# Softmax shift by a scaled minimum, and four order edges between attention and gMLP, in a one-core encoder block

## Chip, core and metric

The kernel runs on one core of one Trainium2 chip. The metric is the device time of one execution in microseconds (us), lower is better. PE is TensorE (matrix products; PEld its weight loads), DVE is VectorE, ACT is ScalarE, POOL is GpSimd; SP is SyncE, which here only issues transfers.

## What is computed

One layer of an encoder on a sequence of 512 positions and 1024 features, in float32. The change touches the attention branch and the gMLP branch. The reference, cut to these:

```python
n = rms_norm(h, norm_mix_pre)
z_gmlp, q, k, v, gates = jnp.split(n @ w_in, split_points, axis=-1)
# gMLP: z -> gelu(z) = [u | v]; LN(v); mixing of positions in chunks of 128
y_a = gmlp_spatial_gating(jax.nn.gelu(z_gmlp), ...)          # u * (W_s LN(v) + b_s)
# attention: 3 groups (dilation 1, 4, 16) of 4 heads, windows of radius 64
s = jnp.einsum('bdnqhe,bdnkhe->bdnhqk', qb, kw) * scale
s = jnp.where(valid, s, MASK_VALUE)
m = jnp.max(s, axis=-1, keepdims=True)
p = jnp.exp(s - m)
denom = jnp.sum(p, axis=-1, keepdims=True)
o = jnp.einsum('bdnhqk,bdnkhe->bdnqhe', p, vw) / denom
lse = (m + jnp.log(denom))[..., 0]
w_mix = jax.nn.softmax(jnp.stack(lses, axis=0), axis=0)      # mixes the 3 groups
y_b = jnp.sum(w_mix[..., None] * o_all, axis=0)
...                                                          # gates, W_out, then the feed-forward part
```

## The kernel before

Every float32 operand of a large product is split in two fp32r halves, `hi` (a copy by ACT) and `lo = x - hi` (a subtraction by DVE), and a product is three matmuls (`mm3`, L94 to L98): hi x hi, hi x lo, lo x hi. `wsplit` (L72 to L79) splits a block of weights; its ACT line is L77 and its DVE line L78. `split_into` (L90 to L92) does the same for activations; `dma_split` (L81 to L88) forms `lo` with two ACT copies and an accumulating transfer issued by POOL.

The stages, in the order of the program:

- Norm of the input, then the attention values of three groups (`token_major`, L267; the tiles `pv` are its four accumulators, 128 positions each).
- Four heads (L671 to L673): `project_qk(h)` and then `mix(h)`. `project_qk` projects q and k for the three groups. `seven_qk` (L424) does it by a seven-product scheme: products 6, 1, 5, 2, 7, 3, 4 of 12 matmuls each into three half banks X, Y, Z, with copies between them: `p1` (ACT, L439) reads X after product 1, `u2` (DVE, L445) adds Y and p1, `z5` (ACT, L447) reads Z, `u3` (DVE, L451) reads Y. Product 2 adds into X, 7 into Y, 3 into Z, so they come after these reads. Then rotary positions (`rotate`), scores (`scores_a` for group 0, `scores_b` for groups 1 and 2 together) and softmax.
- `softmax_tile` (L526 to L533) treats one tile of 128 rows and 256 keys: one DVE operation adds the mask and takes the row maximum `mx` (L529), a second, of one column, forms `nm = -SCALE * mx` (L531), and ACT computes `exp(SCALE * s + nm)` with its row sum (L532). A head has 4 tiles "a" and 4 tiles "b".
- `mix(h)` (L562 to L606) combines the groups: with the row maxima and sums of both kinds it computes factors on a few columns. Two small matmuls with a constant matrix (`pp`, L569, and `pc`, L592) carry numbers between row orders. ACT then scales the four "b" tiles (L598) and, with `ca` (L596), the four "a" tiles (`scale_a`, L602). For heads 0 to 2 `scale_a` is traced during the next head's first `seven_qk` (list `pending`), for the last head at once.
- `attend(h)` transposes the scaled probabilities (L625, L638) and multiplies them with the values into `py` (L655 to L657, L662). It is traced in the middle of the next head. The result of heads 0 to 2 goes to memory (`ybd`, L669) and is loaded back after the heads (`ybh`, `ybl`, L681).
- gMLP: `token_major(COL_V, ...)` (L726) projects the gMLP's values into four accumulators `pv` (8 k x 4 r x 3 = 96 matmuls of 512 columns); their evacuation `evac_v` (L716 to L724) is `gelu2` (ACT square L692, DVE L693, ACT tanh L694, DVE L695), statistics, a power on POOL (`rs_out`, L108) and the normalisation `vln` (L724). Then u (tiles `pf`, L737) is projected group by group, with the steps of the last head's `attend` in between (L728 to L741), and gated with the mixed values (`pg`, L749).
- Gates, branches and W_out, and then the feed-forward part, which is some two thirds of the time.

The order of the instructions on each engine is not that of the program. A scheduler orders them ahead of time with its own estimate of durations, each engine's queue is then fixed, and on the chip each engine works through its queue in that order, waiting for what an instruction needs. `tc.issue_after(x)` adds edges to that: instructions traced inside the block that run on x's engine are put behind x in that engine's queue. It adds no wait on the chip. Transfers issued by POOL or SP stand in those queues as well.

Two buffers matter. The half banks X, Y, Z and the accumulators `pv` come from the same four banks ("acc"), so that the first `pv` matmuls share PE with the last head's projections. And the weight blocks `slab` (the value weights, two of 1 MB), `uw` (u) and `gw` (gates) share three buffers ("raw"), so that a load waits until an earlier block has been split.

Of the kernel before, what the change touches and what calls it, by code (L numbers as in the profile page):

```python
# [10 lines left out]
F32 = mybir.dt.float32  # L11
F32R = mybir.dt.float32r
AF = mybir.ActivationFunctionType
ALU = mybir.AluOpType
PSUM = bass.MemoryType.PSUM

P = 128
S = 512
D = 1024
KD = D // P  # L20
# [4 lines left out]
NH = 4  # L25
SCALE = 1.0 / math.sqrt(HD)
NEG = -1e30
GW = 512
COL_U, COL_V = 0, GW
COL_Q, COL_K, COL_VV, COL_G = 1024, 2560, 4096, 5632  # L30
ROT = 64
# [6 lines left out]
def block_kernel(ctx: ExitStack, tc: tile.TileContext, x, norm_mix_pre, w_in, b_gate, ln_v_gain, ln_v_bias,  # L38
                 w_spatial, b_spatial, w_branch_a, w_branch_b, w_out, norm_mix_post, norm_mlp_pre, w_up,
                 w_down, norm_mlp_post, rope_c, mask_c, perm_c, out):  # L40
    nc = tc.nc
# [30 lines left out]
    def wsplit(raw, pl=None, bufs=None, tag="w", sub=None):  # L72
        pl = pl or wpool
        shape = list(raw.shape)
        hi = pl.tile(shape, F32R, name="hi", tag=tag + "hi", bufs=bufs)
        lo = pl.tile(shape, F32R, name="lo", tag=tag + "lo", bufs=bufs)
        nc.scalar.activation(hi, raw, AF.Copy)  # L77
        (sub or nc.vector).tensor_tensor(lo, raw, hi.bitcast(F32), op=ALU.subtract)  # L78
        return hi, lo  # L79
# [14 lines left out]
    def mm3(ps, a, b, start, stop):  # L94
        (ah, al), (bh, bl) = a, b
        nc.tensor.matmul(ps, ah, bh, start=start, stop=False)  # L96
        nc.tensor.matmul(ps, ah, bl, start=False, stop=False)  # L97
        return nc.tensor.matmul(ps, al, bh, start=False, stop=stop)  # L98
# [38 lines left out]
    start = ExitStack()  # L137
# [126 lines left out]
        for k0 in range(0, nk, kper):  # L264
            yield k0, wload([kper, ncol], lambda r: [(r, wap[k0 * P:(k0 + kper) * P, c0:c0 + ncol].rearrange("(k p) c -> p k c", p=P))], "slab")

    def token_major(c0, stationary, evac, half_way=None):  # L267
        accs = [psA.tile([P, 512], F32, name="pv", tag="acc", bufs=4) for _ in range(4)]
        for k0, raw in slabs(w_in, c0, KD, 512, 4):
            if k0 and half_way:  # L270
                half_way()
            for j in range(0, 4, 2):
                wh, wl = wsplit(raw[:, j:j + 2])
                for jj in range(2):
                    k = k0 + j + jj
                    for r in range(4):
                        mm3(accs[r], (stationary(nh, k, r), stationary(nl, k, r)), (wh[:, jj], wl[:, jj]), k == 0, k == KD - 1)
        for r in range(4):
            evac(r, accs[r])

# [245 lines left out]
    def softmax_tile(h, ab, i, ps, mask):  # L526
        mx = stat[h, "m", ab]
        p = ppool.tile([P, 2, P], F32, name="p")
        nc.vector.tensor_tensor_reduce(p, ps, mask, 1.0, -3.0e38, ALU.add, ALU.max, mx[:, i:i + 1])  # L529
        nm = small.tile([P, 1], F32, name="nm", bufs=8)  # L530
        nc.vector.tensor_scalar(nm, mx[:, i:i + 1], -SCALE, None, op0=ALU.mult)  # L531
        nc.scalar.activation(p, p, AF.Exp, bias=nm, scale=SCALE, accum_out=stat[h, "d", ab][:, i:i + 1])  # L532
        probs[h, ab, i] = p  # L533

    def scores_b(h, got):
# [26 lines left out]
    def mix(h):  # L562
        mda, mdb = stat[h, "md", "a"], stat[h, "md", "b"]
        shape = [P, 2, 4, 4]
        xa = small.tile(shape, F32, name="xa", bufs=2)
        nc.vector.tensor_tensor(xa, mda.unsqueeze(3).to_broadcast(shape), by_r.to_broadcast(shape), op=ALU.mult)
        bank = {"tag": "S", "bufs": 2} if h == NH - 1 else {"tag": "T"}
        pp = psA.tile(shape, F32, name="pp", **bank)
        nc.tensor.matmul(pp, perm[:, 0:P], xa, start=True, stop=True)  # L569
        xb = small.tile(shape, F32, name="xb", bufs=2)  # L570
        nc.vector.tensor_tensor(xb, pp, by_c.to_broadcast(shape), op=ALU.mult)
        mab = small.tile([P, 2, 4], F32, name="mab", bufs=2)
        nc.vector.tensor_reduce(mab, xb.rearrange("p m c r -> p m r c"), axis=mybir.AxisListType.X, op=ALU.add)
        big = small.tile([P, 4], F32, name="big", bufs=2)
        nc.vector.tensor_tensor(big, mab[:, 0], mdb[:, 0], op=ALU.max)
        e = small.tile([P, 2, 4], F32, name="e", bufs=2)
        nc.vector.tensor_tensor(e[:, 0], mab[:, 0], big, op=ALU.subtract)
        nc.vector.tensor_tensor(e[:, 1], mdb[:, 0], big, op=ALU.subtract)
        nc.scalar.activation(e, e, AF.Exp, scale=SCALE)
        z = small.tile([P, 2, 4], F32, name="z", bufs=2)  # L580
        nc.vector.tensor_tensor(z[:, 0], e[:, 0], mab[:, 1], op=ALU.mult)
        nc.vector.tensor_tensor(z[:, 1], e[:, 1], mdb[:, 1], op=ALU.mult)
        nc.vector.tensor_tensor(z[:, 0], z[:, 0], z[:, 1], op=ALU.add)
        nc.vector.reciprocal(z[:, 0], z[:, 0])
        cf = small.tile([P, 2, 4], F32, name="cf", bufs=2)
        nc.vector.tensor_tensor(cf[:, 0], e[:, 0], z[:, 0], op=ALU.mult)
        nc.vector.tensor_tensor(cf[:, 1], e[:, 1], z[:, 0], op=ALU.mult)
        sq = [P, 1, 4, 4]
        xc = small.tile(sq, F32, name="xc", bufs=2)
        nc.vector.tensor_tensor(xc, cf[:, 0:1].unsqueeze(2).to_broadcast(sq), by_c.to_broadcast(sq), op=ALU.mult)  # L590
        pc = psA.tile(sq, F32, name="pc", **bank)
        nc.tensor.matmul(pc, perm[:, P:2 * P], xc, start=True, stop=True)  # L592
        xd = small.tile(sq, F32, name="xd", bufs=2)
        nc.vector.tensor_tensor(xd, pc, by_r.to_broadcast(sq), op=ALU.mult)
        ca = small.tile([P, 4], F32, name="ca", bufs=2)
        nc.vector.tensor_reduce(ca, xd[:, 0], axis=mybir.AxisListType.X, op=ALU.add)  # L596
        for i in range(4):
            nc.scalar.activation(probs[h, "b", i], probs[h, "b", i], AF.Copy, scale=cf[:, 1, i:i + 1])  # L598

        def scale_a():  # L600
            for i in range(4):
                nc.scalar.activation(probs[h, "a", i], probs[h, "a", i], AF.Copy, scale=ca[:, i:i + 1])  # L602
        if h == NH - 1:
            scale_a()
        else:
            pending.append(scale_a)  # L606

    def attend(h):
        for _ in attend_steps(h):
# [80 lines left out]
    def gelu2(ps, dst):  # L690
        t = gpool.tile([P, S], F32, name="gt", bufs=2)
        nc.scalar.activation(t, ps, AF.Square)  # L692
        nc.vector.scalar_tensor_tensor(t, t, 1.0 / GELU_A, ps, op0=ALU.add, op1=ALU.mult)  # L693
        nc.scalar.activation(t, t, AF.Tanh, scale=GELU_C * GELU_A)  # L694
        nc.vector.scalar_tensor_tensor(dst, t, 1.0, ps, op0=ALU.add, op1=ALU.mult)  # L695
# [19 lines left out]

    def evac_v(c, ps):  # L716
        v = vln[:, c]
        gelu2(ps, v)
        st6 = small.tile([P, 6], F32, name="st6")
        nc.vector.bn_stats(st6, v)  # L720
        mv = small.tile([P, 2], F32, name="mv")
        nc.vector.bn_aggr(mv, st6)
        r = rstd_of(mv[:, 1:2], 1.0, 4.0 * EPS)
        normed.append(nc.vector.tensor_scalar(v, v, mv[:, 0:1], r, op0=ALU.subtract, op1=ALU.mult))  # L724

    token_major(COL_V, lambda n, k, c: n[:, k, ROT + c * P:ROT + (c + 1) * P], evac_v)  # L726

    steps = attend_steps(NH - 1, "S", 2)  # L728
    next(steps)
    for g2 in range(2):  # L730
        raw = wload([KD, 2 * P], lambda r: [(r, fcols(w_in, COL_U + g2 * 2 * P, KD, 2 * P))], "uw")
        for j in range(2):
            g = 2 * g2 + j
            wh, wl = dma_split(raw[:, :, j * P:(j + 1) * P], fcols(w_in, COL_U + g * P, KD, P))
            ps = psA.tile([P, S], F32, name="pf", tag="acc" if g else "T", bufs=4 if g else 1)
            for k in range(KD):
                ins = mm3(ps, (wh[:, k], wl[:, k]), (nhn[:, k], nln[:, k]), k == 0, k == KD - 1)  # L737
                if k % 4 == 3 and steps:
                    with tc.issue_after(ins.ins):
                        if next(steps, 0) == 0:  # L740
                            steps = None  # L741
            u = gpool.tile([P, S], F32, name="u", bufs=2)
            gelu2(ps, u)
            if g == 0:
                with tc.issue_after(ins.ins):
                    spatial_weights()
            pg = psA.tile([P, 4, P], F32, name="pg", tag="acc", bufs=4)
            for c in range(4):
                nc.tensor.matmul(pg[:, c], vln[:, c, g * P:(g + 1) * P], wst[:, g], start=True, stop=True)  # L749
            t = gpool.tile([P, 4, P], F32, name="sv")  # L750
            nc.vector.scalar_tensor_tensor(t, pg, cols[:, 16 + g:17 + g], sbias[:, g:g + 1].to_broadcast([P, 4, P]), op0=ALU.mult, op1=ALU.add)
            tf = t.rearrange("p c t -> p (c t)")
            nc.vector.scalar_tensor_tensor(tf, tf, 0.5, u, op0=ALU.mult, op1=ALU.mult)
            split_into(yah[:, g], yal[:, g], tf)
# [585 lines left out]
```

## Time and profile before

| | us |
|---|---|
| median of 3 runs | 775.78 (775.67 to 775.94) |
| profiled execution | 775.82 |
| its span, first to last instruction | 774.0 |
| PE busy | 765.8 (99%) |
| PEld busy | 693.1 (90%) |
| DVE busy | 606.7 (78%) |
| ACT busy | 470.2 (61%) |
| POOL busy | 106.3 (14%) |

The span is shorter than the execution's time by what lies around it (1.8 us). A PE that is busy is not one at its peak: matmuls are pipelined, and how far apart they start depends on their shape and on what stands before them. In rows of the order of time each line gives start, duration, engine, source line, operation, output <- input and, in brackets, the idle time before it and what ended it. In rows of waits: who waited <- for whom: total us, times, longest. In rows of the chain: start, us, what. Starts of PE rows differ by 0.15 us between the order of time and the chain, since the chain counts a matmul from where it takes over the array.

### The profile page before, as it was taken

The numbers are of one execution on the slowest core, as the hardware profiler recorded it, in microseconds if no ns is written. First come the engines' busy times: TensorE is split into PE (matmuls) and PEld (weight loads), VectorE is DVE, ScalarE is ACT, GpSimd is POOL, SyncE is SP. The second block draws the span as 40 slices with busy tenths as digits, with TensorE's granted clock in tenths as the row PEclk, the third lists the DMA queues.
The fourth block names the chain that finished last, engine by engine and source line by source line (L and its number), as shares of the span: only waits on it lengthen the run. The fifth ranks groups of instructions, "written<-read, shape, count | busy, mean of one in ns | idle before, by whom it ended". The sixth has DMA issues, their size and how long they took to land.

```text
span 774.0 us, 12492 instructions
## 1 busy us (share of the span) xinstructions
PE 765.8 (99%) x4903; PEld 693.1 (90%) x4903; DVE 606.7 (78%) x976; ACT 470.2 (61%) x766; POOL 106.3 (14%) x148
## 2 busy tenths in 40 slices
PE   9999999999999999999999999999999999999996
PEld 6888999999998889999998899999999988888885
DVE  7784689888883888778766459998888699978785
ACT  6352468978778674545453557566666766655671
POOL 3300200010103440001000210011211100203010
PEclk9999999999999999999999999999999999999999
DMA  9743744262557993224446323469999988979702
GB/s 311 247 123 113 200 109 110 58 167 77 134 167 138 248 185 83 82 83 135 146 146 209 128 94 124 163 198 290 197 275 223 239 308 308 197 248 213 217 1 108
DMA packets 104348, 131.63 MB, mean 170 GB/s; under 512 B 3393, under 2 KB 73825, under 8 KB 103394
## 3 DMA queue, kind: packets, MB, share of 16 engines
q1 hardware_dynamic: 75472, 79.31, 32.0%
q0 software_dynamic: 28528, 51.15, 28.7%
q8 instruction: 38, 0.62, 0.3%
q10 hardware_dynamic: 290, 0.40, 0.1%
q14 instruction: 20, 0.16, 0.1%
HBM read 120.87 MB, written 26.74 MB: 191 GB/s over the span
## 4 chain that ended last, share of the span: by engine, by line
PE 96%; DMA 2%; DVE 1%; issue 0%; POOL 0%; ACT 0%; POOLq 0%; DVEq 0%; ACTq 0%
PE pacc L1063 13%; PE pg L378 12%; PE pgacc L378 7%; PE pd L1156 6%; PE pd L1154 6%; PE pd L1155 6%; PE ptp L1063 5%; PE pf L96 4%; PE pf L97 4%; PE pf L98 4%; PE pv L97 4%; PE pv L98 4%; PE pv L96 4%; PE pgS L378 3%; PE pd L97 2%; PE pd L96 2%
## 5 line engine op out<-in xcount | busy, mean ns | idle before, releaser
L1155 PE MATMUL pd<-hl,hhl 128*128 128x512 f32 x224 | 87.2, 389 | 0.0
L1156 PE MATMUL pd<-hl,hhl 128*128 128x512 f32 x224 | 87.0, 389 | 0.0
L1154 PE MATMUL pd<-hl,hhl 128*128 128x512 f32 x224 | 84.7, 389 | 0.0
L1063 PE MATMUL pacc<-nt,hl 128*128 128x256 f32 x504 | 66.1, 279 | 0.0
L1063 PEld LDWEIGHTS pacc<-nt,hl 128*128 128x128 f32 x504 | 62.0, 188 | 0.1
L77 ACT ACTIVATE hi<-s 128x1024 fp32r<-128x1024 f32 x34 | 35.9, 1059 | 36.7 <-DVE s L362 11.7
L1156 PEld LDWEIGHTS pd<-hl,hhl 128*128 128x128 f32 x224 | 42.0, 188 | 8.8
L1155 PEld LDWEIGHTS pd<-hl,hhl 128*128 128x128 f32 x224 | 42.0, 188 | 8.8
L78 DVE TENSOR_TENSOR lo<-s,hi 128x1024 fp32r<-128x1024 f32 x34 | 41.5, 1224 | 10.6 <-ACT hi L77 10.3
L1154 PEld LDWEIGHTS pd<-hl,hhl 128*128 128x128 f32 x224 | 42.0, 188 | 8.6
L91 ACT ACTIVATE hl<-s 128x1024 fp32r<-128x1024 f32 x28 | 29.4, 1057 | 26.0 <-DVE s L1046 18.7
L92 DVE TENSOR_TENSOR hl<-dnw,hl 128x1024 fp32r<-128x1024 f32 x32 | 38.5, 1223 | 7.5 <-ACT hl L91 7.5
L1063 PE MATMUL pacc<-n,hl 128*128 128x256 f32 x336 | 44.1, 279 | 0.0
L91 ACT ACTIVATE hl<-dnw 128x1024 fp32r<-128x1024 f32 x32 | 33.0, 1054 | 18.0 <-DMA dnw<-in_w_down_dram 5.6
L1063 PEld LDWEIGHTS pacc<-n,hl 128*128 128x128 f32 x336 | 41.3, 188 | 0.0
L378 PE MATMUL pg<-nt,hi 128*128 128x256 f32 x216 | 39.8, 281 | 0.0
L92 DVE TENSOR_TENSOR hl<-s,hl 128x1024 fp32r<-128x1024 f32 x28 | 34.2, 1222 | 5.2 <-ACT hl L91 5.2
L1144 DVE TENSOR_TENSOR hhl<-hid,hhl 128x1024 fp32r<-128x1024 f32 x24 | 29.3, 1223 | 10.9 <-ACT hhl L1143 10.7
L97 PE MATMUL pv<-lo,nh 128*128 128x512 f32 x96 | 37.4, 390 | 0.0
L1143 ACT ACTIVATE hhl<-hid 128x1024 fp32r<-128x1024 f32 x24 | 25.2, 1055 | 20.0 <-PE pd L1156 20.0
L96 PE MATMUL pv<-hi,nh 128*128 128x512 f32 x96 | 37.3, 395 | 0.0
L98 PE MATMUL pv<-hi,nl 128*128 128x512 f32 x96 | 36.9, 391 | 0.0
(407 smaller groups left out, 2323.6 us busy)
## 6 DMA issues: line engine op xcount, KB each, us to landing
upw<-in_w_up_dram SPq DMA_DIRECT2D x16, 1024.0 KB, 6.4
qkw<-in_w_in_dram SPq DMA_DIRECT2D x24, 512.0 KB, 5.2
dnw<-in_w_down_dram SPq DMA_DIRECT2D x12, 1024.0 KB, 7.0
gw<-in_w_in_dram SPq DMA_DIRECT2D x16, 512.0 KB, 5.4
t3d<-in_w_down_dram POOLq DMA_DIRECT2D x8, 1024.0 KB, 9.0
t1d<-in_w_down_dram POOLq DMA_DIRECT2D x8, 1024.0 KB, 9.1
slab<-in_w_in_dram SPq DMA_DIRECT2D x6, 1024.0 KB, 11.7
tsum<-in_w_down_dram POOLq DMA_DIRECT2D x6, 1024.0 KB, 9.4
```

Of the source, the lines that this page charges most:

```text
L77: nc.scalar.activation(hi, raw, AF.Copy)
L78: (sub or nc.vector).tensor_tensor(lo, raw, hi.bitcast(F32), op=ALU.subtract)
L91: nc.scalar.activation(hi, src, AF.Copy)
L92: return sub.tensor_tensor(lo, src, hi.bitcast(F32), op=ALU.subtract)
L96: nc.tensor.matmul(ps, ah, bh, start=start, stop=False)
L97: nc.tensor.matmul(ps, ah, bl, start=False, stop=False)
L98: return nc.tensor.matmul(ps, al, bh, start=False, stop=stop)
L378: nc.tensor.matmul(ps, a[:, j], b[:, j], start=first and not (j or i), stop=(j == KH - 1 and i == 2), skip_group_check=True)
L1063: ins = nc.tensor.matmul(ps, a[:, j], b[:, j], start=first and not (j or m), stop=(j == KH - 1 and m == 2), skip_group_check=True)
L1154: nc.tensor.matmul(ps, ah, bh, start=start, stop=False, skip_group_check=True)
L1155: nc.tensor.matmul(ps, ah, bl, start=False, stop=False, skip_group_check=True)
L1156: return nc.tensor.matmul(ps, al, bh, start=False, stop=stop, skip_group_check=True)
```

## The change

`softmax_tile` now computes `-SCALE * (s + mask)` and its row minimum in the one DVE operation, so `mx` holds minus the scaled maximum and goes straight into the exponential as its bias, with scale -1; `nm` is gone. `mix` works with these numbers: the larger maximum is now the smaller `mab` or `mdb`, and the exponential has scale -1.

Four edges are added: in the gMLP's value projection the first half split (L77, k0 = 0, j = 0) goes behind the last `scale_a` operation of head 2 on ACT (`behind[0]`); the matmuls of k = 7 go behind the `pc` matmul of the last head's `mix` on PE; the two ACT operations of `gelu2` in `evac_v` go behind the last `scale_a` operation of the last head; and the first u product goes behind the last value product on PE (`ended`).

```diff
-    def token_major(c0, stationary, evac, half_way=None):
+    ended = []
+
+    def token_major(c0, stationary, evac, half_way=None, behind={}):
...
             for j in range(0, 4, 2):
-                wh, wl = wsplit(raw[:, j:j + 2])
+                with tc.issue_after(behind[k0 + j].ins) if k0 + j in behind else nullcontext():
+                    wh, wl = wsplit(raw[:, j:j + 2])
                 for jj in range(2):
                     k = k0 + j + jj
                     for r in range(4):
-                        mm3(accs[r], (stationary(nh, k, r), stationary(nl, k, r)), (wh[:, jj], wl[:, jj]), k == 0, k == KD - 1)
+                        with tc.issue_after(behind[k, r].ins) if (k, r) in behind else nullcontext():
+                            ended[:] = [mm3(accs[r], (stationary(nh, k, r), stationary(nl, k, r)), (wh[:, jj], wl[:, jj]), k == 0, k == KD - 1)]
...
-        nc.vector.tensor_tensor_reduce(p, ps, mask, 1.0, -3.0e38, ALU.add, ALU.max, mx[:, i:i + 1])
-        nm = small.tile([P, 1], F32, name="nm", bufs=8)
-        nc.vector.tensor_scalar(nm, mx[:, i:i + 1], -SCALE, None, op0=ALU.mult)
-        nc.scalar.activation(p, p, AF.Exp, bias=nm, scale=SCALE, accum_out=stat[h, "d", ab][:, i:i + 1])
+        nc.vector.tensor_tensor_reduce(p, ps, mask, -SCALE, 3.0e38, ALU.add, ALU.min, mx[:, i:i + 1])
+        nc.scalar.activation(p, p, AF.Exp, bias=mx[:, i:i + 1], scale=-1.0, accum_out=stat[h, "d", ab][:, i:i + 1])
...
-        nc.vector.tensor_tensor(big, mab[:, 0], mdb[:, 0], op=ALU.max)
+        nc.vector.tensor_tensor(big, mab[:, 0], mdb[:, 0], op=ALU.min)
...
-        nc.scalar.activation(e, e, AF.Exp, scale=SCALE)
+        nc.scalar.activation(e, e, AF.Exp, scale=-1.0)
...
-        nc.tensor.matmul(pc, perm[:, P:2 * P], xc, start=True, stop=True)
+        second = nc.tensor.matmul(pc, perm[:, P:2 * P], xc, start=True, stop=True)
...
             for i in range(4):
-                nc.scalar.activation(probs[h, "a", i], probs[h, "a", i], AF.Copy, scale=ca[:, i:i + 1])
+                scaled_a[h] = nc.scalar.activation(probs[h, "a", i], probs[h, "a", i], AF.Copy, scale=ca[:, i:i + 1])
+            mixed_c[h] = second
...
-        gelu2(ps, v)
+        with tc.issue_after(scaled_a[NH - 1].ins):
+            gelu2(ps, v)
...
-    token_major(COL_V, lambda n, k, c: n[:, k, ROT + c * P:ROT + (c + 1) * P], evac_v)
+    token_major(COL_V, lambda n, k, c: n[:, k, ROT + c * P:ROT + (c + 1) * P], evac_v,
+                behind={0: scaled_a[NH - 2], **{(7, r): mixed_c[NH - 1] for r in range(0, 4)}})
...
-                ins = mm3(ps, (wh[:, k], wl[:, k]), (nhn[:, k], nln[:, k]), k == 0, k == KD - 1)
+                with nullcontext() if g or k else tc.issue_after(ended[0].ins):
+                    ins = mm3(ps, (wh[:, k], wl[:, k]), (nhn[:, k], nln[:, k]), k == 0, k == KD - 1)
```

More of the change, by code (lines that the diff above doesn't have):

```diff
@@ L606, in mix @@
             pending.append(scale_a)
+    scaled_a, mixed_c = {}, {}
     def attend(h):
```

## The prediction

> **What bounds the kernel now.** I read the busy times of the page first, then the stages (the busy time of each engine in chosen windows), then the waits of TensorE (PE), and then only the stretch from 200 to 265 us, in which all the edited code runs, by the chain of waits and by the order of time.
>
> ```profile
> span 774.0 us, 12492 instructions
> PE 765.8 (99%) x4903; PEld 693.1 (90%) x4903; DVE 606.7 (78%) x976; ACT 470.2 (61%) x766; POOL 106.3 (14%) x148
> 120.00:205.00 85.00, 85.00 (x639) 81.02 (x638) 73.30 (x202) 68.69 (x151) 3.85 (x5) 1.00 0.40 108
> 205.00:280.00 75.00, 74.78 (x472) 66.34 (x471) 54.40 (x138) 57.08 (x113) 25.30 (x27) 1.00 0.82 181
> 280.00:765.00 485.00, 485.00 (x3135) 442.51 (x3134) 387.37 (x512) 282.13 (x400) 55.33 (x74) 1.00 0.63 178
> PE pg L749 <- DVE vln L724: 0.2, 1, 0.2
> ```
>
> Rows 3 to 5 are stages (us from the span's start): length, then busy time of PE, PEld, DVE, ACT and POOL, then the granted clock. From 120 us to 765 us, PE stands still for 0.22 us in all, at one place (the last row: the spatial gating's product `pg`, L749, waits for the normalised values `vln`). The edits touch the attention heads (120 to 250 us) and the gMLP (210 to 270 us). There the matmuls are queued nose to tail, and no edit adds or removes a matmul. So what the change can win by taking waits away is 0.22 us. What else it can move is the price of the order itself: a matmul that follows one of another kind is dearer.
>
> ```profile
> 247.26 0.23 PE pv L98
> 247.49 0.13 PE pc L592 x2
> 247.62 0.33 PE pv L96
> ```
>
> These are slots in the chain of waits. A `pv` matmul takes a slot of 0.23 us, and the one behind the two small `pc` matmuls takes 0.33: a switch back costs 0.10 us. If a new order has three switches more or fewer, the time moves by 0.3 us.
>
> **Softmax minimum.** Each of 4 heads has 8 softmax tiles; each loses one small operation on VectorE (DVE), `nm`.
>
> ```profile
> L531 DVE TENSOR_SCALAR nm<-mda x16: 144/146/151, 124.9 to 231.7; 128x1 f32<-128x1 f32 x16
> L531 DVE TENSOR_SCALAR nm<-mdb x16: 145/148/151, 129.6 to 238.4; 128x1 f32<-128x1 f32 x16
>   ACT p L532: 5.8, 4
> L529 DVE CUSTOM_DVE_ANT_0 p<-psb,masks x16: 415/421/425, 128.3 to 238.0; 128x256 f32<-128x256 f32 x16
> ```
>
> 32 x 0.147 = 4.7 us of DVE work goes (less, where they overlap), and ACT's exponentials (L532) lose a releaser for which they waited 5.8 us in all, 4 times. PE waits for neither: the stage 120 to 205 us has PE at 85.00 of 85.00. Worth 0.0 us of the end, and the cover is PE's queued projections. The reduction itself stays one operation of the same shape, with another constant, another reducing operation and another start value; no row shows this form. Nearest is its own 0.42 us. If it cost as much again, 32 x 0.42 = 13.4 us more on DVE, 78% busy, over 115 us: hidden by the same matmuls until a head's chain is longer than its cover, so 0 to +1 us; if it were cheaper, 0. I take 0.42 and 0. The change of sign in `mix` (minimum for maximum, scale -1) keeps the count: 0. Had the cover not been there, up to the 4.7 us would be won; this is the size of what is *not* won.
>
> **Weight split behind the scaling (the only edge that moves something in the order of before).** ACT now may start the first split `hi` of the value weights (L77) only after the four scalings `scale_a` of head 2 (L602).
>
> ```profile
> 210.92 1.06 ACT L77 ACTIVATE hi<-slab 128x1024 fp32r<-128x1024 f32 x1 [2.31 <-PE pg L378]
> ...
> 215.57 0.38 ACT L439 ACTIVATE p<-pg 128x256 f32<-128x256 f32 x1
> 215.85 1.70 ACT L602 ACTIVATE p<-p,ca 128x256 f32<-128x256 f32 x4
> 212.01 1.23 DVE L78 TENSOR_TENSOR lo<-slab,hi 128x1024 fp32r<-128x1024 f32 x1 [0.55 <-ACT hi L77]
> 214.19 0.17 DVE L596 TENSOR_REDUCE ca<-xd 128x4 f32<-128x16 f32 x1
> 215.48 0.23 PE pv L96
> ...
> 216.87 0.71 PE pg L378 x6
> ```
>
> Before, the split is at 210.92 and the scaling at 215.85. Taking the 1.06 us away at 210.92 lets what is queued behind it on ACT move up by as much at most: the scalings of the other half (L598), and p1 (L439), whose end is 215.95 now. `ca` is there at 214.36, so the scaling can begin at about 214.9 rather than 215.85. Then the first split: about 216.6 to 217.6 on ACT, its `lo` on DVE (1.23) until about 219. So `pv` can run from about 219 and not from 215.48. Six `pv` matmuls that stood at 215.48 to 216.87 (1.39 us) must be replaced there. What follows them at 216.87 is product 2 of the last seven-product projection. It adds into the bank that p1 reads, so it needs p1's end. If p1 keeps its place, PE waits from 215.48 to 215.95, 0.5 us; if ACT moves up by its 1.06, p1 ends at 214.9 and the wait is 0. I take 0, as the moved instruction stood ahead of p1 on the same engine, and ACT's idle time in the profile is marked at L77 (2.31 us) and at none of the rows behind it. Behind it stand products 7, 3 and 4 of the same projection (12 slots of 0.71 / 6 us, 1.42 each); with product 2 that is 5.7 us of PE work from 215.48, until 221.2, and `pv` is ready at 219. The other end, +3.7 us, is rival 1.
>
> No DMA is moved by name. The SP queue's next loads wait for the slab's buffer, though:
>
> ```profile
> slab<-in_w_in_dram SPq DMA_DIRECT2D x6, 1024.0 KB, 11.7
> 215.65 4.51 SPq L69 DMA_DIRECT2D uw<-in_w_in_dram  x2
> 251.85 1.06 ACT L85 ACTIVATE hi<-uw 128x1024 fp32r<-128x1024 f32 x1
> ```
>
> The two `uw` issues span 215.65 to 220.16; the second (some 219.8) goes into the buffer of the first slab, once both its halves are split. If that is 1 us later, the load is 1 us later, and its first half is wanted at 251.85. With the 11.7 us that a load of this size took at the median, 20 us of slack are left: 0.
>
> **The last four products, the evacuation, and the first u product.** Three other edges: matmuls of k = 7 behind `pc` of the last mixing; GELU's two ACT operations behind the last scaling; the first `u` product behind the last `pv`. All three hold already:
>
> ```profile
> 247.33 0.29 PE L592 MATMUL pc<-xc,perm 128*128 128x16 f32 x2
> 248.93 0.39 PE L96 MATMUL pv<-hi,nh 128*128 128x512 f32 x1
> 251.65 0.39 PE L96 MATMUL pf<-nh,hi 128*128 128x512 f32 x1
> 243.19 0.17 DVE L590 TENSOR_TENSOR xc<-cf,perm 128x16 f32<-128x16 f32 x1
> 248.07 1.71 ACT L602 ACTIVATE p<-p,ca 128x256 f32<-128x256 f32 x4 [0.18 <-DVE ca L596]
> 249.81 0.60 ACT L692 ACTIVATE gt<-pv 128x512 f32<-128x512 f32 x1
> ```
>
> The 12 matmuls of k = 7 are the last 12 of `pv`, 248.93 to 251.65, and `pc` is at 247.33; GELU's square (249.81) is behind the scaling (to 249.78); `pf` is behind the last `pv`. These edges fix an order that stood there by itself. Queued behind them: the 12 matmuls, then everything on PE. The price if `pc` came late: its input is ready at 243.36 and it stands at 247.33, 4.0 us of slack, so 0. Bounds: 0, to a wait of as long as `pc` slips beyond that slack.
>
> **The one wait.** The 0.22 us goes back through POOL's queue:
>
> ```profile
> 250.10 9.16 DMA ybd<-yb
> 259.55 0.77 POOL ybh L681
> ...
> 261.10 0.59 POOL rs_out L108
> 261.71 0.56 DVE vln L724
> 262.31 0.49 PE pg L749 x2
> ```
>
> `vln` is held up by `rs_out`, which stands in POOL's queue behind two loads that wait for head 2's `ybd` to be written. Head 2's scaling now comes about 1 us earlier, so its output can too: the wait goes, -0.2 us; if the order stays as it is, 0. I take -0.2, since the scaling is the first link of that chain.
>
> **Sum** against the profiled execution (775.82: its span 774.0 and 1.8 around it; 0.04 above the median of 775.78): 0.0 (softmax) + 0.0 (split) + 0.0 (three edges) - 0.2 (wait), with 0.3 either way for switches: 775.6, against the median as well.
>
> Were this wait to grow instead, to the 4 us of rival 2, the rows would price it at 4 us, at the clock of 1.00 that each stage above was granted. The Trainium skill (TensorE: Matmul & The Clock Gate, Part 1) says that an idle window of about 3.4 us halves TensorE's clock until it has been busy about as long again; by that rule, as an estimate, such a wait would cost 4 + 1.7 = 5.7 us, and rival 2 end near 781.5. No wait of this trace between 120 and 765 us is longer than 0.2 us, so no row here shows it.
>
> **Rivals.**
> 1. *The moved `pv` matmuls were the cover, and nothing takes their place* (slower). Place: 215.48 to 223.9. Besides the six, ten more stand between the products there:
>
> ```profile
> 220.14 0.24 PE pv L96
> 221.81 0.23 PE pv L96
> ```
>
> (one at 220.14, and nine from 221.81, up to 223.9). So if every product keeps its time, 16 x 0.23 = 3.7 us of idle time appear before `pv` starts, with nothing won back, since PE's work is the same. It decides (over 1.55 us) when more than 7 of the 16 slots stay empty. For: the products need p1, u2, z5 and u3 from ACT and DVE, and ACT's rows above stand close. Against: ACT and DVE are relieved of 1.06 and 1.23 us just ahead. Middle of 1.55 and 3.7: 778.4. Under that point it gives 776.0 to 777.3.
> 2. *`pg` is queued earlier on PE while `rs_out` stays behind the `ybd` write* (slower). The order is made anew from the program; if GELU looks earlier to it, `pg` may stand where 250.10 + 9.16 us have not yet passed, and the 0.22 us become 1 to 4: 776.7 to 779.7, in the middle 778. Against: the edge holds GELU back just where it stands.
> 3. *The new order is simply smoother* (faster). 0.22 us and 5 to 8 switches fewer: 774.8 to 775.1. To be over 1.55 us it needs 13 switches fewer, which the same heads with the same operations do not offer.
> 4. *The minimum is not free*: the new form costs more on DVE; hidden, 775.7 to 776.7.
>
> **How the numbers follow.** The forecast (within 0.6 us of the sum) 0.58; rival 1 0.17, of it 0.10 over 1.55 us; rival 2 0.06, of it 0.04; rival 3 0.14, of it 0.04 beyond 1.55 us; rival 4 0.05. A measurement of this kernel tells about 0.2% (1.55 us) from no change: faster 0.04, slower 0.14, same 0.82. The time of the likeliest is 775.6. The range takes in rival 3 down to 774.8 and rivals 1 and 4 up to 777.0, leaving out about 0.05 below and 0.15 above.
>
> **What would show it.** Right: PE still at 75 of 75 us between 205 and 280; no row `nm`; the first slab `hi` on ACT behind L602; the first `pv` 3 to 4 us later; `pc`, the scaling and GELU in their old order. Wrong: a wait PE `pg` L378 <- ACT p1 (or z5) near 216 to 222 (rival 1), a longer PE `pg` L749 <- `vln` (rival 2), a reduction L529 over 0.45 us (rival 4). My prediction is wrong as a whole if PE's order changes far from these places, between 120 and 200 us, where I saw no reason for it.

## The result, and the profile after

The changed kernel is slower: 780.25 us at the median of 6 runs (778.96 to 780.52) against 775.74 (775.50 to 776.02), a ratio of 1.0056 [1.0046, 1.0067]. The prediction was 775.6, within 774.8 to 777.0. The profiled execution took 780.24 us, and its span is 4.3 us longer than before. One of the eleven executions of E5 below took 1278.19 us at a mean granted clock of 0.557, and E5's numbers leave it out. The head of the page after:

```profile
span 778.3 us, 12463 instructions
PE 767.8 (99%) x4903; PEld 694.8 (89%) x4903; DVE 603.9 (78%) x944; ACT 469.7 (60%) x766; POOL 105.6 (14%) x148
```

PE has the same 4903 matmuls, DVE 32 operations fewer: `nm` is gone, and nothing came of it. The waits of PE after (who <- for whom: total us, times, longest):

```profile
PE pd L96 <- DVE gs L414: 2.1, 1, 2.1
...
PE pc L594 <- DVE xc L592: 0.6, 1, 0.6
...
PE pg L382 <- ACT p L443: 0.2, 1, 0.2
```

(The rows left out belong to the kernel's start: one of 1.0 us, two of 0.2.) Four of its stages (length, busy time of PE, PEld, DVE, ACT, POOL, granted clock):

```profile
120.00:205.00 85.00, 85.00 (x638) 81.09 (x637) 72.99 (x180) 70.30 (x156) 3.85 (x5) 1.00 0.38 98
205.00:280.00 75.00, 74.26 (x469) 65.89 (x468) 51.37 (x128) 54.91 (x106) 25.19 (x27) 1.00 0.83 190
400.00:460.00 60.00, 57.94 (x300) 49.47 (x299) 31.91 (x55) 25.30 (x52) 8.61 (x17) 1.00 0.42 141
530.00:610.00 80.00, 80.00 (x682) 80.00 (x681) 67.77 (x99) 53.00 (x75) 13.55 (x19) 1.00 0.92 243
```

The last two stages before:

```profile
400.00:460.00 60.00, 60.00 (x323) 51.86 (x322) 34.60 (x60) 27.84 (x56) 9.62 (x18) 1.00 0.42 149
530.00:610.00 80.00, 80.00 (x688) 80.00 (x687) 67.08 (x96) 53.02 (x74) 13.34 (x19) 1.00 0.92 236
```

The two waits of the attention (0.6 and 0.2) stand where the edges were put. The largest one, 2.1 us, stands at 408 us, about 150 us behind every edited line: the first W_out product `pd` waits for the last join of the gates. (The gates use a seven-product projection like that of q and k; its last join, L410 before and L414 after, adds up from the half bank Y and writes a piece of `gs`.) And in the feed-forward part, from 530 to 610 us, PE is busy all the time and still issues six matmuls fewer.

The chain after, at the 2.1 us:

```profile
407.43 0.24 PE pf L98
...
407.86 0.51 issue
408.37 2.35 DVE wo L92 x2
410.72 0.35 DVE gs L414
411.07 0.04 issue
411.11 0.50 PE pd L96
```

The chain before, at the same place:

```profile
406.63 1.40 PE pgacc L378 x12
408.03 0.23 PE pd L96
408.26 0.23 PE pd L97
```

And DVE before, in order of time:

```profile
407.35 2.35 DVE L92 TENSOR_TENSOR wo<-wow,wo 128x1024 fp32r<-128x1024 f32 x2
409.61 0.42 DVE L410 SCALAR_TENSOR_TENSOR gs<-pgacc,p 128x256 f32<-128x256 f32 x1
```

This is the reading that matters. Before, the join also stands behind two splits of W_out's weights, and it also starts (409.61) later than PE's first `pd` (408.03). DVE's queue is no worse after. What differs is the bank. The gates' half banks and the four W_out accumulators take the same four banks ("acc") in turn. The bank numbers in the programs show which accumulator gets the bank that the join still has to read: the fourth before, and the first after. PE fills the first with its first product and comes to the fourth after 27 matmuls (27 x 0.227 = 6.1 us), when the join is long done.

For the sum I take five stretches of PE, each from the start of one matmul to the start of another (us; the first, the 1201st, the first `pd`, the first of the feed-forward part, the first of its last product, the last), since PE has the same matmuls in each:

| kernel, profile | first to 1201st | to first `pd` | to feed-forward | to its last product | to the end |
|---|---|---|---|---|---|
| before | 193.83 | 213.05 | 45.34 | 162.04 | 152.16 |
| after, first | 194.22 | 215.90 | 45.49 | 162.93 | 152.11 |
| after, second | 193.93 | 215.90 | 45.45 | 162.05 | 152.15 |
| after, third | 193.63 | 215.89 | 47.06 | 162.03 | 152.11 |

(The second and third profile are E12 and E13 below.) +2.85 us by the first `pd` comes in every execution. +0.89 before the last product (the six missing matmuls) and +1.6 behind the wait come in some. The first stretch moves by 0.6 us between profiles of one kernel, and that is start-up.

### The profile page after: what moved, and what is told of

The parts are those of the page before. It is cut to its first block, busy times and chain, and to the rows that moved or that the text cites. A ratio compares the mean times of both kernels' runs of the same rounds, so it can differ in the third digit from the quotient of the medians.

```text
span 778.3 us, 12463 instructions
## 1 busy us (share of the span) xinstructions
PE 767.8 (99%) x4903; PEld 694.8 (89%) x4903; DVE 603.9 (78%) x944; ACT 469.7 (60%) x766; POOL 105.6 (14%) x148
## 4 chain that ended last, share of the span: by engine, by line
PE 97%; DVE 1%; ACT 1%; issue 1%; POOL 0%; POOLq 0%; DVEq 0%; ACTq 0%
PE pacc L1071 13%; PE pg L382 11%; PE pgacc L382 7%; PE pd L1163 6%; PE pd L1162 6%; PE pd L1164 6%; PE ptp L1071 5%; PE pf L97 4%; PE pf L96 4%; PE pf L98 4%; PE pv L97 4%; PE pv L96 4%; PE pv L98 4%; PE pgS L382 3%; PE pd L96 2%; PE pd L98 2%
## 5 line engine op out<-in xcount | busy, mean ns | idle before, releaser
L77 ACT ACTIVATE hi<-s 128x1024 fp32r<-128x1024 f32 x34 | 35.9, 1057 | 36.1 <-DVE s L366 11.8
```

## The experiments

Theory: the wait of 2.1 us is a matter of whose turn a bank is, and has nothing to do with the minimum, the splits or the edges as such. Rivals: the minimum or one of the edges costs the time where it stands; or PE reaches W_out in another state.

**E1: after, with the bank's turn moved by one.** A small tile of the spatial gating takes its place from another buffer. PE's order stays but for eight matmuls, all between 259 and 279 us, and the join's bank becomes that of the third accumulator.

```diff
-        pt = psA.tile([P, 32], F32, name="ptr", tag="acc", bufs=4)
+        pt = psA.tile([P, 32], F32, name="ptr", tag="T")
```

> The changed kernel; one small tile of the gMLP (ptr, L706) takes its bank from another tag, so that the four banks 'acc' rotate by one from there on. Bank theory: the first W_out accumulator no longer lands in the bank from which the last gate product is still to be read, the 2.1 us wait of PE at L96 falls away and the time is 780.25 - 2.1 = 778.1 us, with the waits at p1 (0.2) and pc (0.6) as in the changed kernel. Rival theory, lateness carried over from the reordered stretch at 205 to 280 us: this stretch is left as it is, so the wait stays and the time is 780.2.

776.72 us (776.43 to 777.48), 1.0014 [1.0005, 1.0023] of before. Waits of PE:

```profile
PE pc L594 <- DVE xc L592: 0.6, 1, 0.6
...
PE pg L382 <- ACT p L443: 0.2, 1, 0.2
```

No row `pd` is left, and the two local waits are as after. The stretch to the first `pd` is 213.79 us, so 2.11 shorter than after and 0.74 longer than before. The time fell by 3.5 us, more than the wait: what came in addition in some executions was gone too. Some 1.1 us against before stay, with the two local waits.

**E2: before, with the turn moved by two.** Two small transposes into spare tiles of the same banks:

```diff
+        for _ in range(2):
+            spare = psA.tile([P, 32], F32, name="spare", tag="acc", bufs=4)
+            nc.tensor.transpose(spare, rows, ident[:32, :32])
```

> The kernel before, with two spare one-matmul tiles of 32 columns in the gMLP that turn the four banks 'acc' by two places; softmax and order edges as before. Bank theory: now the first W_out accumulator gets the bank of the last gate product, PE waits 2.1 us at L96 before W_out, and the time is 775.7 + 2.1 + 0.2 (the two tiny matmuls) = 778.0. Rival theory (lateness from the reordered stretch, which is not reordered here): 775.7 to 776.0 and no such wait.

779.41 us (779.26 to 781.61), 1.0052 [1.0039, 1.0066]. Waits of PE:

```profile
PE pd L96 <- DVE gs L410: 2.1, 1, 2.1
...
PE prs L711 <- ACT wst L709: 0.7, 1, 0.7
```

Two windows behind them:

```profile
411.00:415.00 4.00, 4.00 (x12) 3.16 (x13) 3.23 (x5) 1.08 (x2) 0.00 (x0) 0.62 0.77 263
530.00:610.00 80.00, 80.00 (x681) 80.00 (x681) 67.74 (x99) 53.06 (x74) 14.11 (x21) 1.00 0.92 244
```

The kernel before, with not one of the change's parts, now has the change's 2.1 us, and nearly its time. (0.7 us are a wait of its own, behind the spare transposes, and some 90 of PE's matmuls change places between 258 and 296 us.) With E1 this shows the bank's turn to be the cause of the 2.1 us. In this execution the granted clock also fell behind the wait (0.62 in the mean of four us), and the feed-forward part had 681 matmuls.

**E3 and E4: each half of the change alone.** E3 has the softmax minimum without the four edges, E4 the edges with the old maximum and `nm`.

> Only the softmax minimum, none of the four edges. Bank theory: the last gate product's bank falls to the second W_out accumulator, which is used 9 matmuls (2.05 us) later, so at most 0.2 us of wait are left: 775.7 to 776.3, less whatever 4.7 us of DVE work are worth, which I put at 0. If the minimum itself costs (a dearer form of the reduction): rows of L529 over 0.45 us and a time of 778 or more.

> Only the four edges, the softmax as before. Bank theory: the last gate product's bank falls to the fourth W_out accumulator, as in the kernel before, so no wait there; what remains is the split moved behind the scaling: 0.2 to 0.5 us at product 2 of the last projection, 776.0 to 776.3. If the edges are what costs the 4.5 us: 779 to 780.

E3: 776.00 us (775.80 to 776.39), 1.0004 [0.9995, 1.0013]. E4: 776.34 (775.64 to 777.18), 1.0009 [1.0000, 1.0017]. Neither list of waits has a row for the join. Each alone is within 0.1% of before, and both together cost 0.56%: the sum of two parts that do nothing. In E3 the join's bank is the second accumulator's, which PE reaches with its tenth matmul, and there it shows in the chain of E3, as one slot of 0.49 us:

```profile
409.38 0.23 PE pd L98
409.60 0.49 PE pd L96
410.09 0.24 PE pd L97
```

In E4 it is the fourth's, as before.

**E5 and E6: after, with the join moved forward on DVE.** W_out's splits from the sixth (E5) or the seventh (E6) on go behind the last join. PE's queue and its banks are those of after; two rows of DVE's change.

```diff
-                nc.vector.scalar_tensor_tensor(c2[:, A], Y, -1.0, p1, op0=ALU.mult, op1=ALU.subtract)
+                joined[:] = [nc.vector.scalar_tensor_tensor(c2[:, A], Y, -1.0, p1, op0=ALU.mult, op1=ALU.subtract)]
...
-                split_into(*wos[-1], raw[:, j])
+                with tc.issue_after(joined[0].ins) if k0 + j >= 5 else nullcontext():
+                    split_into(*wos[-1], raw[:, j])
```

> The changed kernel with two DVE rows moved: the splits of W_out's blocks 5 to 7 go behind the last join of the gates (L414 of the changed kernel), so that this join no longer stands behind two splits of 1.2 us; the order on PE and the bank stay. Theory: PE's wait at the first W_out product shrinks from 2.1 us to what the join itself needs after the last gate product, 0.2 + 0.4 + 0.1 = 0.7 us; the time falls by at least 1.4 us, to 778.9, and by 2.4, to 777.9, if the slower matmul rhythm that the changed kernel shows from 530 to 610 us (0.118 against 0.117 us, 0.95 us in all) hangs on the wait. Rival (the wait only stands for lateness of DVE that comes from earlier): no change, 780.2.

> As e5, but one split (1.2 us) stays ahead of the join. Theory: a wait of about 1.1 us, 1.0 us less than in the changed kernel and 0.4 more than in e5: 779.2, or 778.3 if the slower rhythm goes with the wait. Rival: 780.2.

E5: 777.58 us (777.34 to 778.03), 1.0017 [1.0008, 1.0026]. E6: 778.15 (777.71 to 778.44), 1.0027 [1.0017, 1.0037]. DVE of E5:

```profile
408.89 0.42 DVE L416 SCALAR_TENSOR_TENSOR gs<-pgacc,p 128x256 f32<-128x256 f32 x1 [0.64 <-PE pgacc L382]
409.23 3.48 DVE L92 TENSOR_TENSOR wo<-wow,wo 128x1024 fp32r<-128x1024 f32 x3
```

The wait fell to 0.5 us in E5 and to 0.9 in E6. With the bank unlucky, PE always waits for the join; how long is set by the splits ahead of it. The 0.5 us are what the last product, the join itself and the hand-over take.

**E7: before, nine matmuls later at W_out.** This asks whether arriving 2 us late is enough for what happens in the feed-forward part. Nine 512-column matmuls more ahead of the first `pd`, no wait.

> The kernel before with nine more matmuls of 512 columns ahead of the first W_out product (their sums are overwritten), so that PE gets to everything behind them 9 x 0.227 = 2.04 us later, but without standing still. If lateness alone brings the slower rhythm from 530 to 610 us: 775.6 + 2.04 + 0.95 = 778.6, with 0.118 us from matmul to matmul there. If it takes PE's standing still: 777.7, with 0.117.

778.13 us (777.82 to 779.23), 1.0028 [1.0018, 1.0037]: 9 x 0.227 = 2.0 us and no more, with 688 matmuls from 530 to 610.

**E8: after, without the edge of the k = 7 matmuls.** The program gives the join the bank of the fourth accumulator here, so I expected the 2.1 us to go.

```diff
-                behind={0: scaled_a[NH - 2], **{(7, r): mixed_c[NH - 1] for r in range(0, 4)}})
+                behind={0: scaled_a[NH - 2]})
```

> The changed kernel without the edge that puts the matmuls of k = 7 behind pc. Two things at once, by the order in the queues: the last gate product's bank falls to the fourth W_out accumulator (no wait there), and PE no longer waits 0.6 us for pc. Theory: 780.25 - 2.3 - 0.95 - 0.6 = 776.4. If the edge were harmless where it stands and something else made the loss: 779 to 780.

779.92 us (779.71 to 781.46), 1.0053 [1.0041, 1.0066], a miss by 3.5 us. The wait at `pd` is gone, as it should be, but PE now has these waits between 255 and 267 us:

```profile
PE py L660 <- ACT ptah L91: 1.2, 1, 1.2
...
PE prs L713 <- ACT wst L711: 0.7, 1, 0.7
PE pt L643 <- DVE ptal L92: 0.3, 1, 0.3
```

and in the window behind the first of them the clock fell, to 0.77 in the mean:

```profile
262.00:268.00 6.00, 5.31 (x25) 4.42 (x25) 5.28 (x15) 4.01 (x8) 2.67 (x3) 0.77 1.24 278
```

Without the edge the twelve `pv` matmuls run earlier (until 252.0 us instead of 253.2), the u products move up behind them and ahead of `pc`, and between the last head's first transposes and their products no filler is left. The stretch from the 1201st matmul to `pd` is 217.24 us, 4.2 more than before; part of that is the lower clock. So beside the other edges this one is worth more than it costs. That it repairs what the first edge does is likely, but no run took out the first edge alone.

**E9 and E10: before, with PE made to stand still, its banks unchanged.** One more matmul ahead of the first `pd` reads a split of W_out's weights that is not ready (the seventh in E9, a later one on DVE in E10). This separates the standing still from the bank.

> The kernel before, banks and queues as they are, with one more 512-column product ahead of the first W_out product, which reads the seventh split of W_out's weights: PE has to stand still there, by the times of those splits in the profile before for about 1.7 us. It tells standing still from the bank: in the kernel after and in the second experiment a wait of 2.1 us at this place went with a slower rhythm of the matmuls between 525 and 615 us (0.1178 us from start to start instead of 0.1167, about 0.95 us in all) and once with a drop of the granted clock. Theory A (any standing still of this length brings the slower rhythm): 775.8 + 1.7 + 0.95 = 778.4, and 682 matmuls of the window 530 to 610 us instead of 688. Theory B (the rhythm belongs to the order of PE's queue in those kernels and not to the wait): 777.5 and 688. With a drop of the granted clock some runs are 1.7 us longer.

> As the ninth, but the added product reads the split of W_out's weights after the next two go by, about 3 us of standing still by the profile before (it ends at 411.2 us there, PE is ready at 408.0). Theory A: 775.8 + 3.1 + 0.95 = 779.9, with the slower rhythm; theory B: 778.9, without it. If standing still is what makes the granted clock fall, then this one falls more often than the second experiment did (one execution in several), and its time is 780.5 to 781.6 in most runs; the profiled run shows a granted clock of 0.5 for some 3.4 us right behind the wait.

E9: 778.40 us (777.90 to 778.65), 1.0032 [1.0019, 1.0045], with 688 matmuls from 530 to 610 us. In its profile PE is 2.2 us later from there to the end (1.9 of standing still, 0.34 for the added matmul), and the rest of the 2.6 us by which its span is longer lies ahead of it. E10: 780.86 (779.29 to 781.79), 1.0063 [1.0050, 1.0077], with 688 as well. E10's PE in order of time:

```profile
410.83 0.80 PE L935 MATMUL pd<-wo,mh 128*128 128x512 f32 x1 [3.19 <-DVE wo L92]
411.43 0.63 PE L96 MATMUL pd<-hi,mh 128*128 128x512 f32 x1
411.85 0.63 PE L97 MATMUL pd<-lo,mh 128*128 128x512 f32 x1
412.28 0.63 PE L98 MATMUL pd<-hi,ml 128*128 128x512 f32 x1
```

The starts are 0.43 us apart instead of 0.23: the clock fell, in this profile, and in four of the five times by their size. So a longer stop brought the clock down, and a stop by itself need not bring the slower feed-forward part. Theory A (any stop brings it) was wrong here. Theory B (it belongs to the order of PE's queue) fits these two runs and falls with E12 to E15 below.

**E11: the best that the runs point to.** The minimum alone (E3) with E5's edit, so that the 0.26 us at the tenth matmul go too.

> The softmax minimum alone (the third experiment, 776.0), with the splits of W_out's weights from the sixth on queued behind the last join of the gates, which moves two instructions of VectorE and none of another engine. In the third experiment the tenth W_out product began 0.26 us late because of that join. Theory (that lateness is all that stands between the minimum alone and the kernel before): 775.7. Rival (the minimum's saved 4.7 us of VectorE are worth something once nothing stands in their way): 775.3 or less. Rival (the order of the two splits and the join doesn't matter at 0.26 us): 776.0.

776.04 us (775.67 to 776.85), 1.0003 [0.9994, 1.0012]. The slot of 0.49 is gone (from `pd` to the feed-forward part 45.34 us, E3 had 45.62), and the time does not tell it from E3 or from before. The minimum is free, and worth nothing that the time can tell.

**E12 to E15: the same kernels again.** E12 and E13 are the kernel after, E14 is E2, E15 is E5, each for one more profile: does the slower part belong to a kernel or to an execution?

> The kernel after once more, unchanged. Its six times fall into two groups, 778.96 and 779.45, and 780.24 to 780.52, and its one profile had the slower rhythm of the 256-column matmuls (682 in the window from 530 to 610 us). Theory A (the rhythm comes out anew in each execution): the times fall into groups about 0.95 us apart, and a further profile may show 688. Theory B (the rhythm belongs to this kernel's queues and times): each profile shows 682 or 683, and the spread of the times is the start of the kernel and the drop of the granted clock.

> As the twelfth, for one more profile. Theory A: 682 or 688 in the window from 530 to 610 us; theory B: 682 or 683 again.

> The second experiment's kernel once more, for a profile: the wait of 2.1 us at the first W_out product has to be there again. Theory A: 682 or 688 matmuls in the window from 530 to 610 us; theory B: 682 or 683. The granted clock falls to 0.5 behind the wait in some executions and in others not.

> The fifth experiment's kernel once more, for a profile: 0.5 us of wait at the first W_out product. Theory A: 682 or 688 matmuls in the window from 530 to 610 us; theory B: 688 again.

E12: 779.30 us (778.99 to 780.79), 1.0051 [1.0037, 1.0065]. The single times were E13 780.26, E14 781.22, E15 778.14. The window 530 to 610 us of E12:

```profile
530.00:610.00 80.00, 80.00 (x688) 80.00 (x687) 68.22 (x100) 53.14 (x73) 13.14 (x19) 1.00 0.93 243
```

of E13, with the one behind the wait:

```profile
411.00:415.00 4.00, 4.00 (x13) 3.16 (x12) 3.23 (x5) 0.86 (x2) 0.00 (x0) 0.60 0.69 238
530.00:610.00 80.00, 80.00 (x688) 80.00 (x687) 68.39 (x99) 53.37 (x75) 14.31 (x20) 1.00 0.93 247
```

and of E15:

```profile
530.00:610.00 80.00, 80.00 (x682) 80.00 (x681) 67.39 (x97) 52.71 (x73) 12.49 (x18) 1.00 0.91 238
```

The kernel after had 682 once and 688 twice. E2's kernel had 681 and then 688 (E14), and E5's had 688 and then 682 (E15). So the slower rhythm comes out anew in each execution, which is theory A of E12 to E15. The clock's fall does as well: none in the first two profiles of after, one in the third. The 12 times of after fall into two groups, five from 778.96 to 779.45 and seven from 780.24 to 780.79. The first profile's 780.24 had the slow rhythm and the third's 780.26 the fallen clock; the second's 779.10 had neither.

## Why the prediction was wrong, point by point

- **The step that failed: a missing term, at the border 150 us away.** The sum had terms for the places of the edits and none for what PE's first product in the next stage waits for: the 485 us from 280 to 765 us, in which PE never stood still before, were put at nothing. The runs show 2.1 us there instead, the wait for the join. The prediction named this as its own refutation ("wrong as a whole if PE's order changes far from these places"), and that is what happened: PE's order after differs from that before from 130.6 us, in the heads, to 330.7; 623 of its 4903 places hold another matmul. It is the minimum that does this to the heads, since E3's order differs from 130.6 us on as well and E4's only from 215.3. The minimum shortens a chain, the scheduler lays out the heads anew, with the edges on top the banks' turns come out unluckily, and at 408 us this costs 2.1 us. Against before, the stretch from the 1201st matmul to `pd` is 2.85 us longer, and E1 gives 2.11 of these back without touching an edit. The row that could have warned stands in the profile before: the join at 409.61, behind PE's start of `pd` at 408.03, reading a bank from a set that both stages share. A list of waits shows what was late, not what was nearly late.
- **Softmax minimum, 0.0: right.** Of the reduction, one row of after (least, middle and longest ns, first and last start):

```profile
L533 DVE CUSTOM_DVE_ANT_0 p<-psb,masks x16: 414/419/425, 128.7 to 243.4; 128x256 f32<-128x256 f32 x16
```

  0.419 us against 0.421: rival 4 is out. E3 gives 1.0004.
- **First split, 0: a third of a microsecond off, from the step that I chose.** ACT of after, in order of time:

```profile
211.93 0.63 ACT L490 ACTIVATE st<-k 32x512 f32<-32x512 f32 x1 [2.35 <-DVE cf L588]
...
215.58 0.38 ACT L443 ACTIVATE p<-pg 128x256 f32<-128x256 f32 x1
215.90 0.38 ACT L451 ACTIVATE z<-pg 128x256 f32<-128x256 f32 x1
216.18 1.70 ACT L604 ACTIVATE p<-p,ca 128x256 f32<-128x256 f32 x4
217.78 1.05 ACT L77 ACTIVATE hi<-slab 128x1024 fp32r<-128x1024 f32 x1
```

  I took it that ACT moves up by the 1.06 us of the split. It doesn't. Before, `cf` was there at 210.37, and the split held what stood behind it until 211.89. After, the new order brings the exponential `e` at 209.38 instead of 208.40 and `cf` at 211.98, so ACT stands idle for 2.35 us and goes on at 211.93 all the same. `p1` stays at 215.58, and product 2 starts 0.3 us late (0.2 in the list of waits). The rest held: the products filled the places of the moved `pv`, whose first stands at 220.84 (I had 221.2). Rival 1 got its sign and not its size.
- **"All three hold already", with "4.0 us of slack": wrong.** This step too took the old order for granted while the change makes a new one. ACT of after:

```profile
246.22 0.60 ACT L91 ACTIVATE yb<-py 128x512 fp32r<-128x512 f32 x1 [1.32 <-PE py L667]
246.71 1.05 ACT L85 ACTIVATE hi<-uw 128x1024 fp32r<-128x1024 f32 x1
247.80 1.06 ACT L86 ACTIVATE lo<-hi 128x1024 fp32r<-128x1024 f32 x1
248.76 0.19 ACT L581 ACTIVATE e<-e 128x8 f32<-128x8 f32 x1
```

  The last head's softmax is 2 to 5 us later (its last reduction starts at 243.4, before at 238.0), and ACT has three operations, 2.5 us of work, ahead of the exponential `e`. So `xc` is ready at about 250.0 instead of 243.4, and the twelve matmuls of k = 7, now held behind `pc`, wait 0.6 us with it. E8 shows the other side: taking this edge away costs more. The stretch from the 1201st matmul to `pd` is 217.24 us there; E1, which has no wait for the join either, has 213.79.
- **The one wait, -0.2: right by luck.** The row `pg` <- `vln` is gone, and rival 2 did not come. But the first link that the prediction named, head 2's scaling about 1 us earlier, did not come either: it starts at 216.18, before at 215.85. POOL's order changed instead. It issues `ybd` at 248.01, and the write lands after 4.5 us (before: 250.10, and 9.2), so the two loads behind it go out at 252.74 instead of 259.55 and no longer hold up `rs_out`.
- **The clock, behind a wait.** In E13 the stretch behind the wait is 47.06 us, in E12 45.45, so a fallen clock cost 1.6 us. The prediction's estimate by the Trainium skill (TensorE: Matmul & The Clock Gate, Part 1) was 1.7, and here the trace agrees. The idle window of about 3.4 us that the same section of the Trainium skill gives does not hold as the length a stop must have. PE stood still for 2.2 us (its starts were 2.33 us apart instead of 0.12) in all five profiles of the kernel after and of E2's, and the clock fell in three of them.

  The traces' records of the granted clock show what sets the three apart. The full clock lasts for whole steps of 3.413 us: in E2, E10, E13 and E14 it falls after 119 of them, in E8 after 75, and for one step each time. The steps begin at another moment in each execution (7.21, 6.51 and 4.56 us from the span's start in the three profiles of after). In the three profiles in which the clock fell, the stop lay in one step (but for 0.15 us in E2), and PE was busy for 1.36 to 1.50 us of that step. In the two in which it stayed, the stop lay across a border, and PE was busy for at least 1.87 us of either step. No sharp limit follows, since the clock stayed in E9 with 1.70 us and fell in E8 with 1.94. The same section of the Trainium skill says that the window runs freely and does not start with the kernel, so that the moment varies from run to run; here the traces agree. The prediction used the rule for its rival 2 alone, as no wait in the trace before was longer than 0.2 us.

The parts that add up, in the first profile of after: 0.4 up to the 1201st matmul, where two further profiles have 0.1 and -0.2; 2.85 to `pd`, which is 2.2 for the join, 0.75 for `pc` and 0.3 for `p1`, less about 0.4 for `vln` and small switches; 0.15; and 0.9 for the rhythm. That is 4.3, the whole. What stays open: what starts the slower rhythm. Standing still (E9, E10) or being late (E7) did not bring it, in one profile each, and no queue decides it, since the same kernel shows both. It was seen in three of the ten profiles with a wait at `pd` and in none of the seven without one (the second profile of a kernel counted by itself); that is too few to say whether the wait invites it.

## What to carry to other kernels

Where a scheduler lays out the queues and buffers are taken in turn, an edit changes the turns of everything behind it. Before costing the edit, look at each border between stages that share buffers for a reader that ends after the next stage has begun: its place in the turn is luck, and a small tile in or out is worth microseconds there. Two parts that did nothing alone cost 0.56% together here, and one tag gave three quarters of it back; so before a change is called bad, move a turn by one. And what one execution does behind a stop need not come in the next, so one profile is too few to tell what a stop costs.

## What the runs showed of the hardware

PE starting every 0.1167 us on 256-column matmuls is not the only steady state: in the same kernel, at a granted clock of 1.00 and with no wait, it also ran for 90 us at one start every 0.1178 us (682 matmuls in 80 us against 688), in a pattern of three matmuls (0.116, 0.118, 0.119) where the second profile has one of four (0.113, 0.116, 0.118, 0.120). A pattern of three by itself is not the slow one, since E11 has it at 0.1167. Which pace an execution gets is settled at the entry of the stage, near 525 us, and lasts until the columns change near 615. It is worth 0.9 us in 776. And the granted clock changes at the borders of steps of 3.413 us, which begin at another moment in each execution. A stop of 2.2 us brought it to half for one step in three profiles of five, those in which the stop fell into one step; one of 1.9 us (E9) did not, in one profile, and one of 3.3 us (E10) did.
